# Gated linear attention by pairs of heads in one direction, with another order of the jobs

## The chip, the cores and the metric

One Trainium2 chip, one of its cores. The metric is the device time in microseconds from launch to end; it is given as the median of the runs shown, and a profile of one execution stands beside it.

## The reference

Two layers of one block, for 512 latent tokens (stream x) and 256 context tokens (stream c), width 1024. Each layer normalises and modulates the tokens, projects them with w_in, runs three mixers side by side, gates each of them, adds them and projects with w_out. The mixers are a convolution of width 31 (with a layer norm), a bidirectional gated linear attention, and grouped attention with 8 query heads. The change is in the linear attention: 4 heads with keys of 64 and values of 128, in chunks of 64 tokens, forwards and backwards:

```
cum = jnp.cumsum(log_a, axis=2)
last = cum[:, :, -1]
q_in = q * jnp.exp(cum)
k_in = k * jnp.exp(-cum)
att = jnp.where(mask, jnp.einsum('bnihd,bnjhd->bnhij', q_in, k_in), 0.0)
o_intra = jnp.einsum('bnhij,bnjhe->bnihe', att, v)
k_state = k * jnp.exp(last[:, :, None] - cum)
contrib = jnp.einsum('bnjhd,bnjhe->bnhde', k_state, v)
decay = jnp.exp(last)
# step over chunks: S <- decay * S + contrib
o_inter = jnp.einsum('bnihd,bnhde->bnihe', q_in, jnp.swapaxes(s_prev, 0, 1))
return (o_intra + o_inter).reshape(b_, t_, h_, dv), s_fin
```

The forward and the backward result are added, normalised, gated and projected with w_gla_out. Context tokens come first in both directions and pass their state on to the latent tokens. The second layer needs no output for the context.

## The kernel before, in words

The kernel is written as many small threads (Python generators) that a planner, the class Weaver (line 106), weaves into one order at build time. The planner keeps a clock for each engine from a price list (Engine.pe, line 251, and Engine.cost, line 273), takes the ready thread that can start first, and records its instructions; on the chip each engine then runs its list strictly in that order. All instructions pass through one helper, line 301, and DMAs through line 319, so that the profile names operations by tile and not by line.

The main thread runs a list of jobs, which the strings P["o0"] and P["o1"] write out by hand for the two layers (from line 78): q0 and q1 are the attention's projections, c0 to c7 the convolution's, v and k those of the linear attention (values; keys and queries), s0 to s11 the branch gates, m0 to m23 the merge gates, a and g (h in layer 1) the modulation of the next layer's input and of the outputs, and two digits a merge job (branch 0 convolution, 1 linear attention, 2 attention; then a block of columns). Projections split their fp32 operands into a high and a low part (hi and lo), in fp32r, and take three products. Loads of weights go ahead of the jobs as buffers become free: raw weights of projections (two buffers), and modulation weights in the general SBUF tiles r3 (29 of them, 128 x 768). Before any job, gates 8 and 9 (KOuter, line 595) run block by block as the first normalised inputs arrive.

PSUM has three pools of two buffers each: pg for projections and merges, pm for transposes, norms and readouts, p2 (double size) for attention and for the products of linear attention. The convolution is 31 multiply-adds over whole rows for each of 4 channel tiles, all on VectorE (tiles r, with the taps tp); it runs in a thread of low priority among everything else.

Linear attention starts when attention is over (gla_bias, line 1458): projections of values and of the low-rank gate, then log gates for all heads, one tile for each head with the 64 channels of the forward direction in partitions 0 to 63 and of the backward one in 64 to 127. The cumulative sum over time is two scans for each head, one of each half and one of them reversed (line 1526). Keys and queries (gla_qk_jobs, line 1533) leave PSUM four times for every projected tile of two heads and stream: each head's 64 rows are written to both halves of its own tile. Two lanes (gla_lane, line 1562) then take the four heads. For one head gla_head (line 1573) computes exponentials on ScalarE, the products with k and q on VectorE, transposes ks on TensorE, and then products (line 1654) issues the contributions of 14 chunks to the state (K=64 tokens, M=128, that is both directions in one product for chunks where both are wanted), and the masked attention blocks (K=64). VectorE updates the state chunk by chunk, 11 times for each direction on 64 partitions, forward and backward in turn (states, line 1629), and masks the blocks (intra, line 1640); GpSimd adds the two directions' blocks. The readout multiplies blocks by values, and queries of both directions at once (K=128) by the states, M=64 tokens at a time. gla_out (line 1700) normalises, transposes and stores to DRAM (ogd), from where the branch threads load it (tiles r from ogd; oad is the attention's).

Of the kernel before, what the change touches and what calls it, by code (L numbers as in the profile page):

```python
# [21 lines left out]
T = NC + NX  # L22
# [21 lines left out]
def _consts():  # L44
# [4 lines left out]
    for v in range(2):  # L49
        for g in range(4):  # L50
# [25 lines left out]
P = dict(vb=4, pko=12, res=2, resg=0, lead=6, pbr=2, tlead=3, nf=2, nbk=3, pconv=8, mlead=3, pmain=4, lcap=7,  # L76
         lcg=26, lat=6, vm=100, am=100, gm=104)
P["o0"] = (
    "c4 g0 m15 m1 q0 q1 m0 s3 s0 m16 m3 c2 m8 m10 m12 c0 k0 m14 c1 c3 m6 c5 k1 v0 m20 g1 s1 v1 c7 m4 k3 c6 "
    "m11 s2 m13 m19 m21 k2 m17 a3 s7 s6 m9 s10 s11 m22 m7 m23 m18 s5 a2 20 22 s4 a1 21 23 m5 m2 10 11 13 12 "  # L80
    "01 00 03 a0 02")
P["o1"] = (
    "q1 q0 c2 c5 c3 c6 m15 s1 s8 m14 s2 m22 m0 c1 c0 k1 m2 s0 s6 m5 m12 m20 s11 c4 c7 v1 s4 v0 s10 m9 s3 m6 "
    "h0 m4 m8 h1 k0 k2 m18 s9 m10 m7 s7 s5 k3 m23 m21 m17 m16 m1 22 23 m3 m13 20 m19 21 02 00 m11 03 10 11 12 "
    "01 13")
# [157 lines left out]
class Engine:  # L243
# [7 lines left out]
    def pe(self, name, a, k):  # L251
# [5 lines left out]
        else:  # L257
# [48 lines left out]
def hybrid_kernel(ctx: ExitStack, tc: tile.TileContext, x, c, ctx_in, c_ctx, norm_g, w_mod, b_mod,  # L306
# [452 lines left out]
    class Layer:  # L759
# [24 lines left out]
        def vec_loads(S):  # L784
# [9 lines left out]
            for d in range(2):  # L794
                o.append((vr[61:65, 64 * d:64 * d + 64], gla_b_gate[l, d].rearrange("(h d) -> h d", d=64)))
# [468 lines left out]
        def attn_pv(S, s, qp, h):  # L1264
# [18 lines left out]
            if S.cnt["attn"] == S.nunits:  # L1283
                W.res, W.lowcap = P["resg"], P["lcg"]
                W.low -= 2 * sum(d.get(2 * t) is not None for d in (S.kk, S.qq) for t in range(2))
# [172 lines left out]
        def gla_bias(S):  # L1458
# [63 lines left out]
            for h in range(GH):  # L1522
# [10 lines left out]
        def gla_qk_jobs(S):  # L1533
            S.kk, S.qq = {}, {}

            def dup(dst, t, col, key):
                def ev(s, cols, ps, fr):
                    if 2 * t not in dst:
                        dst[2 * t] = None
                        yield from (need(("r3", 2)) if "low" in dst else W.need_low(2))  # L1540
                        dst[2 * t], dst[2 * t + 1] = r3([T]), r3([T])
# [517 lines left out]
```

## Time and profile before

| | us |
|---|---|
| median of 3 runs (lowest, highest) | 1473.6 (1471.5, 1474.01) |
| the profiled execution's own time | 1471.48 |
| its span, first to last instruction | 1469.3 |
| TensorE busy, weight loads busy | 1401.7, 1196.5 |
| VectorE busy | 1118.8 |
| ScalarE busy | 597.3 |
| GpSimd busy | 237.8 |
| granted TensorE clock, mean share | 0.995 |

Shares of busy time are averages over a program that has two like halves, one for each layer. In the trace, layer 0's attention runs until about 357 us, its linear attention's heads from 541 to 664, its merges from 666 to 805; in layer 1 attention ends at 1131 us, the heads run from 1251 to 1347, the merges from 1317 to 1417. The page's PE row counts a matmul from its start to a modelled end; matmuls overlap in the array, so that a busy PE is not a PE at its peak. "Idle before" in a row is the time in which an engine stood still just before such instructions, and the name after the arrow is what ended it.

### The profile page before, as it was taken

The page shows a single profiled execution, that of the slowest core. Times are in us where ns is not written, and L with a number is a line of the kernel's source. Part 1 is how long each engine was busy: PE and PEld are TensorE (multiplying, and loading weights), DVE is VectorE, ACT ScalarE, POOL GpSimd, SP SyncE. Part 2 cuts the span into 40 slices and gives each one's busy share as a digit, 9 for nine tenths or more (in the row PEclk, how much of TensorE's full clock was granted, in tenths as well). Part 3 has the DMA queues.
Part 4 walks back from the last instruction along what each step waited for, and adds up shares of the span by engine and source line. Part 5 has one row for each costly group of instructions (what it writes and reads, how often), then busy time and mean ns, then how long its engine had stood idle before and what let it go on. Part 6 is the DMA issues. An engine that isn't in the chain of part 4 may idle for free.

```text
span 1469.3 us, 23375 instructions
## 1 busy us (share of the span) xinstructions
PE 1401.7 (95%) x8788; PEld 1196.5 (81%) x8788; DVE 1118.8 (76%) x1976; ACT 597.3 (41%) x1146; POOL 237.8 (16%) x333
## 2 busy tenths in 40 slices
PE   3999999999999999899999999999999999999998
PEld 2798888888998887787888777888888978778786
DVE  4434976778986999885858476886999999888664
ACT  4422465554225342333523164355554267432220
POOL 1001412221000003232050011412331000021200
PEclk9999999999999999999999999999999999999999
DMA  9732322112422622556556353242233173354752
GB/s 269 210 115 72 95 74 68 39 47 74 128 78 58 180 83 65 191 165 180 194 199 214 120 190 119 72 122 67 56 95 101 51 242 111 111 192 144 253 189 73
DMA packets 219365, 187.46 MB, mean 128 GB/s; under 512 B 15681, under 2 KB 182131, under 8 KB 219253
## 3 DMA queue, kind: packets, MB, share of 16 engines
q1 hardware_dynamic: 218948, 185.87, 41.1%
q8 instruction: 69, 1.13, 0.3%
q14 instruction: 44, 0.35, 0.1%
q10 hardware_dynamic: 304, 0.11, 0.0%
HBM read 151.86 MB, written 34.08 MB: 127 GB/s over the span
## 4 chain that ended last, share of the span: by engine, by line
PE 56%; DVE 10%; POOL 3%; ACT 2%; issue 2%; DMA 2%; SPq 1%; DVEq 0%; POOLq 0%; ACTq 0%
PE pg L301 43%; PE p L301 8%; DVE r L301 6%; PE pm L301 5%; POOL sm L301 2%; DVE wlo L301 2%; ACT r L301 1%; DMA r<-oad 1%; DVE sm L301 1%; SPq L319 1%; DVE tg L301 1%; DMA r<-thd 0%; ACT whi L301 0%; ACT tg L301 0%; DMA r<-in_w_mod 0%
## 5 line engine op out<-in xcount | busy, mean ns | idle before, releaser
L301 PE MATMUL pg<-hx,whi 128*128 128x512 f32 x1504 | 382.1, 397 | 1.6 <-DVE r L301 1.0
L301 PEld LDWEIGHTS pg<-hx,whi 128*128 128x128 f32 x1504 | 275.1, 189 | 57.2 <-issue 1.5
L301 DVE SCALAR_TENSOR_TENSOR r<-r,tp,r 128x768 f32<-128x768 f32 (+29 forms) x240 | 204.3, 902 | 0.2
L301 PE MATMUL pg<-hx,wlo 128*128 128x512 f32 x752 | 195.2, 393 | 0.0
L301 ACT CAST whi<-raw 128x512 fp32r<-128x512 f32 (+1 forms) x194 | 114.5, 620 | 187.7 <-PE pg L301 102.0
L301 DVE TENSOR_TENSOR wlo<-raw,whi 128x1024 fp32r<-128x1024 f32 (+1 forms) x140 | 173.0, 1236 | 17.2 <-ACT whi L301 14.4
L301 PEld LDWEIGHTS pg<-hx,wlo 128*128 128x128 f32 x752 | 138.6, 188 | 28.4 <-issue 0.8
L301 ACT ACTIVATE tg<-pg,hv 128x256 f32<-128x256 f32 (+1 forms) x116 | 71.7, 618 | 188.2 <-PE pg L301 163.4
L301 DVE TENSOR_TENSOR r<-r,r 128x512 f32<-128x512 f32 (+7 forms) x208 | 119.4, 600 | 19.0 <-DMA r<-ogd 8.0
L301 PE MATMUL pg<-r,whi 128*128 128x512 f32 (+1 forms) x576 | 125.7, 359 | 1.5 <-DVE r L301 1.4
L301 POOL TENSOR_SCALAR r<-r,sm 128x768 f32<-128x768 f32 (+1 forms) x80 | 81.4, 1019 | 278.1 <-DVE sm L301 207.9
L301 PEld LDWEIGHTS pg<-r,whi 128*128 128x128 f32 x576 | 95.9, 188 | 19.9 <-DVE r L301 2.6
L301 PE MATMUL pg<-hc,whi 128*128 128x256 f32 x768 | 107.2, 288 | 0.0
L301 PEld LDWEIGHTS pg<-hc,whi 128*128 128x128 f32 x768 | 99.4, 192 | 4.0 <-issue 0.7
L301 PE MATMUL p<-r,r 64*128 64x128 f32 (+2 forms) x672 | 90.5, 309 | 8.3 <-DVE r L301 6.0
L301 DVE TENSOR_TENSOR r<-p,r 128x384 fp32r<-128x384 f32 (+2 forms) x152 | 77.4, 543 | 27.1 <-ACT r L301 22.1
L301 ACT ACTIVATE r<-p,sm 128x768 f32<-128x768 f32 (+1 forms) x80 | 65.4, 818 | 70.5 <-DVE sm L301 65.5
L301 PEld LDWEIGHTS p<-r,r 64*128 64x128 f32 (+1 forms) x672 | 68.6, 189 | 22.5 <-issue 11.9
L301 PE MATMUL pm<-r,r 128*128 128x256 f32 (+4 forms) x672 | 83.3, 283 | 0.4 <-DVE r L301 0.4
L301 DVE CAST whi<-raw 128x512 fp32r<-128x512 f32 (+1 forms) x86 | 36.8, 429 | 60.3 <-PE pg L301 29.7
L301 PE MATMUL pg<-whi,hx 128*128 128x272 f32 (+2 forms) x480 | 82.2, 309 | 0.0
L301 POOL TENSOR_TENSOR r<-r,r 128x512 f32<-128x512 f32 (+1 forms) x33 | 45.2, 1375 | 220.4 <-DVE r L301 123.6
(166 smaller groups left out, 2180.7 us busy)
## 6 DMA issues: line engine op xcount, KB each, us to landing
raw<-in_w_in SPq DMA_DIRECT2D x116, 512.0 KB
r<-in_w_mod SPq DMA_DIRECT2D x64, 192.0 KB
thd<-tg SPq DMA_DIRECT2D x48, 256.0 KB
raw<-in_w_out SPq DMA_DIRECT2D x24, 512.0 KB
r<-thd SPq DMA_DIRECT2D x24, 384.0 KB
r<-in_w_mod SPq DMA_DIRECT2D x16, 384.0 KB
sgd<-tg SPq DMA_DIRECT2D x24, 256.0 KB
r<-thd SPq DMA_DIRECT2D x24, 256.0 KB
```

Source lines behind the costliest of these rows:

```text
L301: return real(*a, **k)
L319: (nc.scalar if q else nc.sync).dma_start(dst, src)
```

## The change

A tile now holds two heads of one direction. The log gates of heads 0 and 1 forwards are one tile, and so on: four tiles as before, with one scan for each over all 128 partitions. Keys and queries of a projected tile, which are two heads anyway, leave PSUM once for each stream, into one tile. gla_pair takes the place of gla_head: a pair of heads works on the two directions as two sets of tiles. The contributions have K=64 tokens and M=64 channels, one product for each head, 22 for each head and layer (8 forward, 8 backward, 6 of both in turn); the state updates run over 128 partitions, 22 for each pair, 8 of one direction in a row, 8 of the other, and 6 in turn. The readout has K=64 and M=64, separately for each direction. The second pair waits until the first one has issued its products (event pair0), and a readout takes both pm buffers at once. The planner's price list has a price for 64x64 products, its parameters P differ, and both job orders are new, of which the diff shows none but the parameters. What is quoted is the core; lines of it that go on alike are left out.

```diff
-P = dict(vb=4, pko=12, res=2, resg=0, lead=6, pbr=2, tlead=3, nf=2, nbk=3, pconv=8, mlead=3, pmain=4, lcap=7,
-         lcg=26, lat=6, vm=100, am=100, gm=104)
+P = dict(vb=4, pko=5, res=0, resg=1, lead=5, pbr=6, tlead=3, nf=3, nbk=4, pconv=13, mlead=3, pmain=4, lcap=11,
+         lcg=15, lat=6, vm=103, am=103, gm=121)
...
             elif rows <= 64:
-                c = 0.106 * n / 128
+                mode = (64, 64 if cols <= 64 else 128)
+                c = (0.06 if cols <= 64 else 0.106) * n / 128
             elif cols <= 64:
...
-                dma(w2r[16 * d:16 * d + 16, :, 64 * d:64 * d + 64],
-                    gla_w_gate[l, d].rearrange("r (h e) -> r h e", e=64))
+                dma(w2r[16 * d:16 * d + 16, 2 * d:2 * d + 2],
+                    gla_w_gate[l, d].rearrange("r (p c) -> r p c", c=128))
...
-            for h in range(GH):
+            for h in (0, 2, 1, 3):
                 yield "V"
                 V.tensor_sub(zn[h], cum[h], zn[h])
                 yield "V"
-                V.tensor_tensor_scan(cum[h][0:64], smask[0:64], zn[h][0:64], 0.0, op0=ALU.mult, op1=ALU.add)
-                V.tensor_tensor_scan(cum[h][64:128, ::-1], smask[64:128], zn[h][64:128, ::-1], 0.0,
-                                     op0=ALU.mult, op1=ALU.add)
+                if h < 2:
+                    V.tensor_tensor_scan(cum[h], smask, zn[h], 0.0, op0=ALU.mult, op1=ALU.add)
+                else:
+                    V.tensor_tensor_scan(cum[h][:, ::-1], smask, zn[h][:, ::-1], 0.0, op0=ALU.mult, op1=ALU.add)
...
-                            cp(dst[2 * t + e][64 * o:64 * o + 64, cols], ps[r], None, S.vv[r, col + t:col + t + 1])
+                    if t not in dst:
...
+                    cp(dst[t][:, cols], ps, None, S.vv[:, col + t:col + t + 1])
...
-                h = S.gq.pop(0)
-                yield from wait(S.E(("cum", h)), S.E(("kk", h)), S.E(("qq", h)))
-                yield from S.gla_head(h)
+                p = S.gq.pop(0)
+                if p:
+                    yield from wait(S.E("pair0"))
+                yield from wait(S.E(("cum", p)), S.E(("cum", 2 + p)), S.E(("kk", p)), S.E(("qq", p)))
+                yield from S.gla_pair(p)
...
+            yield from need(("r3", 6))
+            st = [[r3([6, 128]) for _ in range(2)] for _ in range(2)]
+            at = [r3([6, 128]) for _ in range(2)]
...
+            parts = ([(0, i) for i in range(8)], [(1, i) for i in range(8)], [(d, i) for i in range(8, 11) for d in range(2)])
+            chain = [_Event() for _ in parts]
...
+            def states(b, con):
+                if b == 2:
+                    yield from wait(chain[0], chain[1])
+                for n, (d, i) in enumerate(parts[b]):
+                    o = seq[d]
+                    yield "V" if n == 0 else "+V"
+                    V.scalar_tensor_tensor(ST(d, o[i + 1]), ST(d, o[i]), dec[d][:, o[i]:o[i] + 1], con[d, i],
+                                           op0=ALU.mult, op1=ALU.add)
                 free("p2")
...
             def products():
-                for b in range(max(len(groups), 2)):
-                    yield from need(("p2", (b < 2) + (b < len(groups))))
+                for b in range(3):
+                    yield from need(("p2", 1))
                     yield "P" if b == 0 else "+P"
...
+                    pcn = p2([2, 4, 128])
+                    cnt, con = [0, 0], {}
+                    for d, i in parts[b]:
+                        cix = seq[d][i]
+                        e = cix % 2
+                        con[d, i] = pcn[:, e, cnt[e]]
+                        cnt[e] += 1
+                        for a in range(2):
+                            PE.matmul(con[d, i][half[a]], lhsT=kt[d][half[e], cix // 2, half[a]],
+                                      rhs=gv[a][half[e], cix // 2], start=True, stop=True)
+                    spawn(states(b, con), 3)
                     if b < len(groups):
                         tts = groups[b]
-                        pa = p2([2, 4, 128])[:, :, 0:len(tts)]
+                        yield from need(("p2", 1))
+                        yield "+P"
+                        pa = p2([2, 4, 128])
                         for i, tt in enumerate(tts):
                             tk = slice(tt * 128, tt * 128 + 128)
...
+                            for d in range(2):
+                                for a in range(2):
+                                    PE.matmul(pa[:, a, 2 * d + i], lhsT=ki[d][half[a], tk], rhs=em[d][half[a], tk],
+                                              start=True, stop=True)
...
+                free("r3", 4)
+                fire(S.E(f"pair{p}"))
...
-                yield from need(("pm", 1))
+                yield from need(("pm", 2))
...
-                po = pm([nt, 128])
+                po = [pm([nt, 128]) for _ in range(2)]
...
-                    PE.matmul(po[:, i], lhsT=at[:, tt], rhs=gv[h][:, tt], start=(i == 0), stop=False)
-                for i, tt in enumerate(tts):
-                    for e in range(2):
-                        cix = 2 * tt + e
-                        PE.matmul(po[64 * e:64 * e + 64, i], lhsT=qq[h][:, cix * 64:cix * 64 + 64],
-                                  rhs=ST(cix, slice(0, 128)), start=False, stop=(i == nt - 1))
+                    for d in range(2):
+                        for a in range(2):
+                            for e in range(2):
+                                cix = 2 * tt + e
+                                PE.matmul(po[a][64 * e:64 * e + 64, i], lhsT=em[d][half[a], cix * 64:cix * 64 + 64],
+                                          rhs=ST(d, cix)[half[a]], start=False, stop=(i == nt - 1 and d == 1))
                 yield "+P"
-                spawn(S.gla_out(h, s, po, nt), 2)
+                for a in range(2):
+                    spawn(S.gla_out(2 * p + a, s, po[a], nt), 2)
```

Where the instructions stand, first on TensorE, in layer 0, at the products of the first head before (p_902 holds contributions, p_903 attention blocks, pg_ are projections; an x is a count of equal instructions):

```order
L301 MATMUL pg_5762<-hx_330,whi_5512 128x512
L301 MATMUL pg_5762<-hx_329,whi_5512 128x512
L301 MATMUL p_902_5778<-r_693_3978,r_873_5619 128x128 x8
L301 MATMUL p_903_5787<-r_858_5468,r_875_5621 128x128 x4
L301 MATMUL pg_5762<-hx_330,whi_5512 128x512
L301 MATMUL pg_5762<-hx_329,whi_5512 128x512
```

and at those of the first pair now, behind the 16 contributions of the forward chunks (p_881) and the first four of eight attention blocks (p_882); p_883 holds the backward chunks' contributions:

```order
L302 MATMUL p_882_5507<-r_835_5184,r_837_5186 128x128 x2
L302 MATMUL p_882_5507<-r_836_5185,r_838_5187 128x128 x2
L302 MATMUL pg_5470<-hx_331,whi_5271 128x512
L302 MATMUL pg_5470<-hx_330,whi_5271 128x512
L302 MATMUL pg_5470<-hx_331,whi_5271 128x512
L302 MATMUL pg_5470<-hx_330,whi_5271 128x512
L302 MATMUL pg_5470<-hx_331,whi_5271 128x512
L302 MATMUL pg_5470<-hx_330,whi_5271 128x512
L302 MATMUL pg_5470<-hx_331,whi_5271 128x512
L302 MATMUL pg_5470<-hx_330,whi_5271 128x512
L302 MATMUL pg_5470<-hx_331,whi_5271 128x512
L302 MATMUL p_883_5534<-r_714_4115,r_834_5183 64x128
```

Eight contributions of 128 rows became 16 of 64 rows, the blocks of two heads stand together, and nine matmuls of a projection stand between them and the next contributions, which come back to a p2 buffer that p_881 or p_882 must have left.

The state updates on VectorE at the same places, before (r_896 and r_897 are the states, mask the first blocks):

```order
L301 SCALAR_TENSOR_TENSOR r_896_5763<-r_896_5763,sm_5623,p_902_5778 64x128 x7
L301 SCALAR_TENSOR_TENSOR r_897_5764<-r_896_5763,sm_5623,p_902_5778 64x128
L301 SCALAR_TENSOR_TENSOR r_896_5763<-r_896_5763,sm_5623,p_902_5778 64x128
L301 SCALAR_TENSOR_TENSOR r_897_5764<-r_897_5764,sm_5623,p_902_5778 64x128
L301 SCALAR_TENSOR_TENSOR r_897_5764<-r_896_5763,sm_5623,p_902_5778 64x128
L301 SCALAR_TENSOR_TENSOR r_897_5764<-r_897_5764,sm_5623,p_902_5778 64x128
L301 COPY_PREDICATED zt_213<-mask,p_903_5787 128x512
```

and now:

```order
L302 SCALAR_TENSOR_TENSOR r_830_5151<-r_822_5081,tp_233,r_830_5151 128x773
L302 SCALAR_TENSOR_TENSOR r_873_5472<-r_873_5472,sm_5190,p_881_5488 128x128 x5
L302 SCALAR_TENSOR_TENSOR r_874_5473<-r_873_5472,sm_5190,p_881_5488 128x128
L302 SCALAR_TENSOR_TENSOR r_874_5473<-r_874_5473,sm_5190,p_881_5488 128x128 x2
L302 COPY_PREDICATED zt_213<-mask,p_882_5507 128x512
L302 COPY_PREDICATED zt_215<-mask,p_882_5507 128x512
L302 SCALAR_TENSOR_TENSOR r_820_5055<-r_406_2369,tp_233,r_820_5055 128x774
L302 SCALAR_TENSOR_TENSOR r_875_5474<-r_875_5474,sm_5191,p_883_5534 128x128 x3
```

Twelve updates of one head, forward and backward in turn, became eight of two heads in one direction; conv taps (tp) stand between the chains.

The loads on SyncE's queue at the start, before (w_mod 128x3x128 x2 is a modulation load of layer inputs, 128x3x256 one of an output gate; each of the two forms stands six and three times for a job):

```order
L319 DMA r_112_596<-in_w_mod 128x3x128 x2
L319 DMA r_113_599<-in_w_mod 128x2x128 x2
L319 DMA r_114_605<-in_w_mod 128x3x256
L319 DMA r_115_607<-in_w_mod 128x3x256
L319 DMA r_116_609<-in_w_mod 128x2x256
L319 DMA r_127_704<-in_w_mod 128x3x256
L319 DMA r_128_706<-in_w_mod 128x3x256
L319 DMA r_129_708<-in_w_mod 128x2x256
L319 DMA cst<-in_k_const 128x512
```

and now:

```order
L320 DMA r_113_599<-in_w_mod 128x2x128 x2
L320 DMA r_114_605<-in_w_mod 128x3x128 x2
L320 DMA r_115_608<-in_w_mod 128x3x128 x2
L320 DMA r_116_611<-in_w_mod 128x2x128 x2
L320 DMA r_128_705<-in_w_mod 128x3x128 x2
L320 DMA r_129_708<-in_w_mod 128x3x128 x2
L320 DMA r_130_711<-in_w_mod 128x2x128 x2
L320 DMA r_131_718<-in_w_mod 128x3x256
L320 DMA r_132_720<-in_w_mod 128x3x256
L320 DMA r_133_722<-in_w_mod 128x2x256
L320 DMA r_145_820<-in_w_mod 128x3x256
L320 DMA r_146_822<-in_w_mod 128x3x256
```

Six loads of job a2 moved ahead of those of the output gate (g0 before, g1 now) and of the constants.

## Rows read from the trace of the kernel before

**Rows 1.** The page: busy us, share and count, and busy tenths in 40 slices.
```profile
PE 1401.7 (95%) x8788; PEld 1196.5 (81%) x8788; DVE 1118.8 (76%) x1976; ACT 597.3 (41%) x1146; POOL 237.8 (16%) x333
...
PE   3999999999999999899999999999999999999998
...
DVE  4434976778986999885858476886999999888664
```

**Rows 2.** Windows: busy us (count) of each engine, granted clock, DMA share, GB/s.
```profile
450.00:540.00 90.00, 89.00 (x562) 78.10 (x561) 80.74 (x92) 39.47 (x65) 0.40 (x2) 1.00 0.39 113
540.00:620.00 80.00, 71.42 (x513) 61.04 (x512) 73.19 (x126) 26.83 (x48) 20.96 (x35) 0.96 0.36 116
620.00:700.00 80.00, 75.14 (x607) 63.14 (x606) 58.23 (x122) 29.55 (x53) 21.61 (x37) 1.00 0.56 173
...
1240.00:1320.00 80.00, 76.12 (x460) 61.81 (x459) 67.84 (x128) 37.88 (x65) 10.10 (x21) 0.98 0.50 153
```

**Rows 3.** Waits of 540:700 and 1240:1320 (us, times, longest), and the timeline's PE.
```profile
PE p L301 <- DVE r L301: 7.1, 4, 3.6
...
PE pm L301 <- DVE t L301: 4.2, 4, 2.0
...
PE p L301 <- DVE r L301: 2.5, 2, 1.9
...
617.49 1.51 PE L301 MATMUL p<-cst,r 128*128 128x128 f32 x6 [3.63 <-DVE r L301]
...
669.78 0.63 PE L301 MATMUL pm<-cst,tg 128*128 128x128 f32 x4 [2.00 <-DVE t L301]
```

**Rows 4.** PE groups by form: count, busy us, mean ns, idle before; last, the chain.
```profile
L301 PE MATMUL pg<-hx,whi 128*128 128x512 f32 x1504 | 382.1, 397 | 1.6 <-DVE r L301 1.0 <-ACT tg L301 0.6
...
L301 PE MATMUL p<-r,r 64*128 64x128 f32 x384 | 27.7, 286 | 5.5 <-DVE r L301 4.9 <-DVE zt L301 0.5
...
L301 PE MATMUL pg<-r,cstat 128*32 128x128 f32 x768 | 26.2, 286 | 5.0 <-DMA r<-in_w_mod 5.0
...
L301 PE MATMUL pm<-r,r 128*128 128x128 f32 x80 | 11.6, 284 | 0.0
L301 PE MATMUL pm<-r,r 128*64 128x128 f32 x160 | 11.4, 280 | 0.0
...
1442.12 2.75 PE pg L301 x12
```

**Rows 5.** Groups by form on VectorE and ScalarE.
```profile
L301 DVE SCALAR_TENSOR_TENSOR r<-r,sm,p 64x128 f32<-64x128 f32 x176 | 60.8, 346 | 5.7 <-PE p L301 0.6
...
L301 DVE TENSOR_TENSOR_SCAN r<-r,r 64x768 f32<-64x768 f32 x16 | 28.0, 1749 | 0.2
...
L301 DVE TENSOR_TENSOR r<-pg,r 128x128 f32<-128x128 f32 x48 | 11.7, 289 | 0.8 <-PE pg L301 0.6
...
L301 DVE TENSOR_SCALAR r<-pg,vv 64x512 f32<-64x512 f32 x9 | 6.7, 749 | 8.3 <-ACT r L301 8.3
...
L301 DVE TENSOR_SCALAR r<-pg,vv 64x256 f32<-64x256 f32 x7 | 3.4, 484 | 1.7 <-ACT r L301 1.2 <-PE pg L301 0.4
...
L301 DVE COPY sm<-r 64x12 f32<-64x12 f32 x16 | 2.6, 165 | 0.1
...
L301 ACT ACTIVATE r<-pg,vv 64x512 f32<-64x512 f32 x23 | 15.7, 683 | 19.8 <-PE pg L301 12.8 <-DVE r L301 6.8
...
L301 ACT ACTIVATE r<-pg,vv 64x256 f32<-64x256 f32 x17 | 8.0, 470 | 5.2 <-PE pg L301 4.0 <-DVE r L301 1.1
```

**Rows 6.** The first 80 us: GB/s in 40 slices of 2 us; the timeline's PE from 62 us.
```profile
GB/s 8 181 284 227 239 251 283 319 343 298 302 285 291 284 304 312 312 312 294 285 301 281 284 302 290 295 293 340 313 379 271 21 0 0 0 8 44 218 0 66
...
62.40 2.16 PE L301 MATMUL pg<-hc,whi 128*128 128x256 f32 x16
...
69.02 1.98 PE L301 MATMUL pg<-hx,wlo 128*128 128x512 f32 x8
70.92 1.30 PE L301 MATMUL pg<-r,cstat 128*32 128x128 f32 x40
```

More of the change, by code (lines that the diff above doesn't have):

```diff
@@ L1284, in attn_pv @@
                 W.res, W.lowcap = P["resg"], P["lcg"]
-                W.low -= 2 * sum(d.get(2 * t) is not None for d in (S.kk, S.qq) for t in range(2))
+                W.low -= sum(d.get(t) is not None for d in (S.kk, S.qq) for t in range(2))
                 S.kk["low"] = S.qq["low"] = True
@@ new lines, in gla_pair @@
+            q0, qs, kk, qq = S.q0, S.qs, S.kk[p], S.qq[p]
+            gv = S.gv[2 * p:2 * p + 2]
+            half = (slice(0, 64), slice(64, 128))
+            yield from need(("r3", 6))
+            ks, em, ki = ([r3([T]) for _ in range(2)] for _ in range(3))
+            lc, dec = [sm() for _ in range(2)], [sm() for _ in range(2)]
+            for d in range(2):
+                cu = S.cum[2 * d + p]
+                c3 = cu.rearrange("p (n c) -> p n c", c=CH)
+                yield "V"
+                V.tensor_copy(lc[d][:, :NCH], c3[:, :, 0 if d else CH - 1])
+                yield "V"
+                V.tensor_sub(ks[d].rearrange("p (n c) -> p n c", c=CH), c3,
+                             lc[d][:, :NCH].rearrange("p (n o) -> p n o", o=1).to_broadcast([128, NCH, CH]))
@@ new lines, in gla_pair @@
+            yield "S"
+            free("r3", 4)
+            kt = [k.rearrange("p (t d) -> p t d", d=128) for k in ks]
+            for d in range(2):
+                yield from need(("p2", 1))
+                yield "P" if d == 0 else "+P"
+                pk = p2([8, 128])
+                for tt in range(6):
+                    PE.transpose(pk[:, tt], ks[d][:, tt * 128:(tt + 1) * 128], K["ident"])
+                yield "E"
+                cp(kt[d], pk[:, 0:6])
+                free("p2")
@@ L1623, in gla_head, with ST @@
+            yield "S"
+            yield from need(("r3", 6))
+            st = [[r3([6, 128]) for _ in range(2)] for _ in range(2)]
+            at = [r3([6, 128]) for _ in range(2)]
+            def ST(d, cix):
+                return st[d][cix // 6][:, cix % 6]
+            G.memset(ST(0, 0), 0.0)
+            G.memset(ST(1, NCC - 1), 0.0)
+            seq = (list(range(NCH)), list(range(NCC - 1, -1, -1)) + list(range(NCH - 1, NCC - 1, -1)))
             done_a = _Event()
-            blks = ([0, 1, 2, 3, 11, 10, 4, 5], [9, 8, 7, 6, 5, 10])
@@ L1626, in gla_head @@
             groups = [S.qtt[g:g + 2] for g in range(0, len(S.qtt), 2)]
-            chain = [_Event(), _Event()]
-            def states(b, pcn, con, i0, i1):
-                if b:
-                    yield from wait(chain[0])
-                for i in range(i0, i1):
-                    for o, r in ((fo, F_), (bo, B_)):
-                        yield "V" if (i == i0 and r == F_) else "+V"
-                        V.scalar_tensor_tensor(ST(o[i + 1], r), ST(o[i], r), dec[r, o[i]:o[i] + 1], con[o[i]][r],
-                                               op0=ALU.mult, op1=ALU.add)
+            parts = ([(0, i) for i in range(8)], [(1, i) for i in range(8)], [(d, i) for i in range(8, 11) for d in range(2)])
@@ L1667, in products @@
                     if b < len(groups):
                         tts = groups[b]
-                        pa = p2([2, 4, 128])[:, :, 0:len(tts)]
+                        yield from need(("p2", 1))
+                        yield "+P"
+                        pa = p2([2, 4, 128])
                         for i, tt in enumerate(tts):
                             tk = slice(tt * 128, tt * 128 + 128)
-                            for d, r in enumerate((F_, B_)):
-                                PE.matmul(pa[:, d, i], lhsT=ki[r, tk], rhs=qq[h][r, tk], start=True, stop=True)
```

151 lines of the change are left out of this document (57 added, 94 removed).

## The prediction

> **What bounds the kernel now.** I read the page's busy times first. TensorE (PE) is busy 95% of the span, VectorE (DVE) 76%, ScalarE (ACT) 41% [rows 1]. That looks like a TensorE-bound kernel in which no other engine matters, but two views correct it. In the slices, PE is at 8 or 9 tenths everywhere after the first one, and DVE is at 9 only in some slices [rows 1]. The windows put those beside the stages: in 540 to 620 us, where layer 0's linear attention runs, PE is busy 71.42 of 80 us while DVE is busy 73.19; in 620 to 700 us PE has 75.14 of 80; in layer 1's linear attention, 1240 to 1320 us, PE has 76.12 of 80 and DVE 67.84 [rows 2]. So PE idles 8.6 + 4.9 + 3.9 us there. The waits name the cause: in 540 to 700 us PE waits 7.1 us for DVE on tiles r and 4.2 us on tiles t, in 1240 to 1320 us 2.5 us on r [rows 3]; the longest, 3.63 us at 617.49, is the transposes of a head waiting for the product of ks and k on DVE [rows 3].
>
> The second correction is that busy is not full pace. The commonest matmul (128x512, 1504 records) takes 382.1 / 1504 = 254 ns of busy time each, but where the chain of waits runs undisturbed 12 of that size take 2.75 us, 229 ns each [rows 4]. About a tenth of PE's busy time is thus slack that the busy share does not show.
>
> **The array's work.** Each fp32 matmul leaves two records. Before, a head and layer has 14 contributions with K=64, M=128 (8 + 6), two attention blocks per token tile with K=64, M=128, and two readouts of the state per token tile with K=128, M=64. Over 4 heads and 2 layers (6 token tiles in layer 0, 4 in layer 1) that is 112, 80 and 80 matmuls, as the counts x384 (112 + 80, doubled) and x160 say [rows 4]. After, a pair has 22 contributions for each of its two heads with K=64, M=64: 176; the readouts have K=64, M=64 and are split by direction: 160; the attention blocks stay at 80. So 224 + 160 records become 352 + 320 = 672. The old ones cost 27.7 / 384 = 72 ns and 11.4 / 160 = 71 ns of busy time per record, 16.2 + 11.4 = 27.6 us together. The trace has no 64x64 product. The two bounds: 72 ns, as for a half-sized product now, gives 672 x 72 = 48.4, +20.8 us; the modulation products, which stand four beside each other in quarters of the columns (128x32), cost 26.2 / 768 = 34 ns per record [rows 4], and give 22.8, -4.8 us. I take -5, since the trace goes by the share of the array: the full-sized fp32 products take 11.6 / 80 = 145 ns per record, the half-sized 72 and the quarters 34 [rows 4]. A 64x64 product is a quarter, and the loops alternate the two heads (two column halves or two row halves) as the modulation alternates its quarters.
>
> The Trainium skill ("TensorE: Matmul & The Clock Gate", section "Wait — 56ns, not 53.3ns?") has a rule against this: with hardware decode off the sequencer spends about 62 ns per matmul, and that becomes the bound once the array's work is shorter. By it 672 records would cost 41.7 us, +14 instead of -5. The modulation row, 34 ns per record over 768 records, disagrees with it for this kernel.
>
> **VectorE and ScalarE.** States: 176 updates of 64 partitions at 346 ns (60.9 us) become 88 of 128 partitions with the same 128 elements per partition. Duration goes by elements per partition: a 128x128 addition from PSUM takes 289 [rows 5]. Bounds 289 and 346 ns; I take 346: 30.4 us saved (35.5 at the other end). Scans: 16 of 64x768 at 1749 ns become 8 of 128x768: 14.0 us. Copies of the last column: 16 become 8 at 165 ns: 1.3 us. The evacuation of k and q: 56 instructions on half the partitions (DVE 6.7 + 3.4 us, ACT 15.7 + 8.0 us [rows 5]) become 14 on all: a quarter of 33.8 us, 25.3 us saved, 7.6 on DVE and 17.7 on ACT at the old split. DVE is relieved of 53 us in all, about half in each layer; products with the gates, masks, transposes and norms keep their number.
>
> What of it lies on the path? Only where PE waits for DVE. All but the states and some of the scans of layer 0 stand before 540 us, where DVE is busy 80.74 of 90 and PE waits 1 us [rows 2]; a faster DVE shifts its later work forward there, conv taps above all, which run among the heads. With some 26 us less in front of it per layer, DVE reaches the heads' products earlier than PE by more than the waits named, so I let them go: 7.1 + 4.2 - 2.0 = 9.3 us in layer 0 (2.0 us is counted below) and 2.5 in layer 1. The array's granted clock was 0.96 of 2.4 GHz in 540 to 620 us and 0.98 in 1240 to 1320 [rows 2], after these idle stretches; at its other level, 1.2 GHz, that is 3.2 + 1.6 = 4.8 us of lost pulses, which I count as won back. Together -17 us, ends 0 and -22 (all 17.4 us of idle time in the three stretches and the clock). What is late next is the loads: branch products on DVE wait for oad and ogd, and POOL's chain of small operations behind each head's norm is unchanged.
>
> **Waits that the pairs add.** The second pair waits for the first one's products, and each chain of 8 updates now runs in one direction, each update reading what the last one wrote. Queued behind on PE are the next contributions, which need the PSUM buffer of the chain before last. The order puts 8 attention blocks and 9 matmuls of 229 ns between: about 3.2 us, against 8 x 346 = 2.8 us of updates. I cost this at nothing; without that cover (a DVE that is busy with conv taps when the products land) it is up to 2.8 us at each of 8 chains, 22 us. SBUF buffers: a pair asks for 6 + 6 where two heads asked for 3 + 3 each, and k and q hold 4 instead of 8; no cost.
>
> **The order of jobs.** At the start two jobs of modulation now stand before the first projection, a2 and g1, where c4 and then g0 stood. SP sends a2's 2 x 2 x 8 x 128 x 128 x 4 bytes, 2.1 MB, more before the constants. The loads ran at some 290 GB/s until 62 us [rows 6], so g1 arrives 7 us later, at about 69. Before, c4 ran from 62.40 to 71.0 us and g0's products began at 70.92 [rows 6]. Now PE must hold m21 until g1 is through, at 71, and has only a2's 64 records (1.95 us) and the rest of gates 8 and 9 to fill the 8.6 us that c4 filled: +5 us, between 0 (if the loads land sooner) and +8. At the end of layer 0, a0 stood among the last merges, and its transposes waited 2.00 us for a linear-attention output to leave its bank [rows 3]; now a0 runs in the middle of the layer: -2. All other moves I cost at nothing, with +-8, since PE has projections left to run beside the heads in both orders.
>
> **Sum:** -5 -17 +5 -2 = -19 us on the profiled execution's 1471.5 us (span 1469.3, 2.2 around it): 1452.5. The median of the runs shown stands 2.1 above that execution: 1454.6, so I say 1455.
>
> **Rivals.** (a) More is won. If PE's pace improves too in the stages where DVE fell behind, a further 15 to 20 us can go: the commonest form alone holds 1504 x 25 ns = 38 us. For it: DVE is near 90% over long stretches; against: half of that slack lies in stages that the change leaves alone. 1455 - 18 = 1437. (b) No change: what PE waited for at the heads is POOL's norm chain and the loads, which come as late as before, and the start takes 5 us: 1455 + 17 = 1472. For it: both stand behind the heads in the trace; against: the waits name DVE. (c) Slower: the 64x64 products cost as much each as the half-sized ones now, because four do not run beside each other. Place: contributions and readouts; price 72 instead of 34 ns per record: 1455 + 26 = 1481. It decides from 34 + 19 / 0.672 = 62 ns on, where the gain is gone. For it: the trace has no product that splits rows and columns at once; against: the rows of 145, 72 and 34 ns. By the skill's 62 ns the time would be 1455 + 19 = 1474, no change; the row of 34 ns speaks against it. (d) Slower by order: the chains of 8 are not covered (22 us) and start and boundaries lose as much as the heads win: 1455 + 24 = 1479.
>
> **How the numbers follow.** My forecast (1445 to 1466) has 0.50, (a) 0.23, (b) 0.09 with the skill's rule 0.02 of it, (c) 0.08, (d) 0.10. No change means within 0.2%, 3 us, about what a measurement of this kernel can tell. Faster: 0.50 + 0.23 = 0.73; same 0.09; slower 0.18. The likeliest case's time is 1455. The range takes in (a) down to 1430 and (d) up to its 1479; (c) and the far edges, under 0.2, stay out.
>
> **What would show it.** In the changed profile: 672 records of M=64 with 23 us of busy time, and not 48; 88 state updates of about 346 ns and 8 scans of 1.75 us; DVE busy about 1065 us; PE idle in the two linear-attention stages down from 17 us to about 5 with a clock of 0.99 or more; first projection at about 71 us. I am wrong if PE still waits for DVE by 10 us there, if DVE's relief is there but PE's idle time has moved to another stage, or if the records of M=64 cost over 60 ns.

## The result and the profile after

The changed kernel takes 1438.7 us (median of 4 runs, 1437.5 to 1439.5) against 1472.6 us (4 runs, 1471.1 to 1474.0) before, beside it on the same chip: a ratio of 0.9765, 95% interval 0.9753 to 0.9778. It is 34 us faster; the forecast was 18.6 us under the 1473.6 shown, 1455, with 1430 to 1479 as its range. The sign and the range held, and the size is that of rival (a).

The profiled execution has a span of 1435.7 us where before it was 1469.3. The page of the changed kernel, busy times and slices of PE, DVE and the granted clock:

```profile
PE 1384.6 (96%) x9076; PEld 1187.9 (83%) x9076; DVE 1059.7 (74%) x1863; ACT 574.3 (40%) x1113; POOL 233.8 (16%) x325
...
PE   3999999999999999999999999999999999999998
...
DVE  4437966689946999963676485877679999997664
...
PEclk9999999999999999999999999999999999999999
```

Against [rows 1], VectorE has 59.1 us less to do and ScalarE 23.0. TensorE's busy time fell by 17.1 us and its idle time (span less busy) from 67.6 to 51.1, by 16.5: together the 33.6 us of span. The mean granted clock rose from 0.995 to 1.000.

The groups by form that answer to [rows 4] and [rows 5]; the last line is the modulation, which the price of a quarter of the array was taken from:

```profile
L302 PE MATMUL p<-r,r 64*64 64x128 f32 x352 | 12.4, 275 | 2.9 <-DVE r L302 2.9
...
L302 PE MATMUL pm<-r,r 64*64 64x128 f32 x320 | 10.1, 273 | 0.0
...
L302 DVE SCALAR_TENSOR_TENSOR r<-r,sm,p 128x128 f32<-128x128 f32 x88 | 28.8, 343 | 2.7 <-PE p L302 0.9
...
L302 DVE TENSOR_TENSOR_SCAN r<-r,r 128x768 f32<-128x768 f32 x8 | 14.0, 1750 | 0.0
...
L302 PE MATMUL pg<-r,cstat 128*32 128x128 f32 x768 | 26.4, 286 | 4.8 <-DVE t L302 4.2 <-DMA r<-in_w_mod 0.6
```

The 672 records of 64x64 products cost 12.4 + 10.1 = 22.5 us, 33.5 ns each. Their mean length in the row, 275 ns, is the time that one is under way and not its cost, since several are under way at once: the busy time over the count is what is to be read.

Windows of the changed kernel. The heads of layer 0 now run from 495 to 613 us, those of layer 1 from 1231 to 1294, so the stretches that answer to [rows 2] lie earlier; the columns are the same:

```profile
405.00:495.00 90.00, 90.00 (x617) 81.20 (x615) 57.99 (x87) 38.05 (x62) 0.35 (x2) 1.00 0.38 113
495.00:575.00 80.00, 76.10 (x677) 65.60 (x676) 76.63 (x107) 23.94 (x45) 22.34 (x33) 1.00 0.48 134
575.00:655.00 80.00, 77.98 (x677) 66.07 (x676) 62.19 (x134) 40.61 (x65) 19.19 (x35) 1.00 0.49 154
1220.00:1300.00 80.00, 75.05 (x665) 60.49 (x664) 73.16 (x132) 32.27 (x53) 20.89 (x33) 1.00 0.41 130
```

PE idles 3.9 + 2.0 + 5.0 = 10.9 us in the three stretches of the heads, where it was 17.3; the clock is 1.00 in all. PE's waits there, first of 495 to 655, then of 1220 to 1300 us (us in total, times, longest):

```profile
PE pm L302 <- DVE t L302: 3.2, 6, 0.9
PE p L302 <- DVE r L302: 1.4, 3, 0.7
...
PE pm L302 <- DVE t L302: 1.5, 2, 1.3
PE p L302 <- DVE r L302: 1.5, 3, 1.0
PE pm L302 <- POOL r L302: 1.0, 1, 1.0
```

In layer 0 the waits for r went from 7.1 to 1.4 us and the longest from 3.6 to 0.7, against [rows 3]. What is left is many short waits.

### The profile page after: what moved, and what is told of

It is laid out like the page before. It is cut to its first block, busy times and chain, and to the rows that moved or that the text cites. A ratio compares the mean times of both kernels' runs of the same rounds, so it can differ in the third digit from the quotient of the medians.

```text
span 1435.7 us, 23778 instructions
## 1 busy us (share of the span) xinstructions
PE 1384.6 (96%) x9076; PEld 1187.9 (83%) x9076; DVE 1059.7 (74%) x1863; ACT 574.3 (40%) x1113; POOL 233.8 (16%) x325
## 4 chain that ended last, share of the span: by engine, by line
PE 50%; DVE 5%; POOL 1%; issue 1%; ACT 1%; DMA 0%; SPq 0%; DVEq 0%; POOLq 0%
PE pg L302 36%; PE p L302 9%; PE pm L302 4%; DVE r L302 3%; POOL sm L302 1%; DVE tg L302 1%; DVE wlo L302 1%; DVE t L302 0%; DMA r<-oad 0%; DVE zt L302 0%; POOL r L302 0%; ACT r L302 0%; ACT tg L302 0%; DVE sm L302 0%; ACT whi L302 0%
## 5 line engine op out<-in xcount | busy, mean ns | idle before, releaser
L302 PE MATMUL pg<-hx,whi 128*128 128x512 f32 x1504 | 385.8, 397 | 0.3 <-DVE r L302 0.3
L302 DVE SCALAR_TENSOR_TENSOR r<-r,tp,r 128x768 f32<-128x768 f32 (+29 forms) x240 | 201.2, 883 | 0.2
L302 DVE TENSOR_TENSOR wlo<-raw,whi 128x1024 fp32r<-128x1024 f32 (+1 forms) x140 | 173.7, 1241 | 17.1 <-ACT whi L302 16.2
L302 DVE TENSOR_TENSOR r<-r,r 128x512 f32<-128x512 f32 (+8 forms) x208 | 119.1, 599 | 24.7 <-DMA r<-ogd 9.0
L302 DVE TENSOR_TENSOR r<-p,r 128x384 fp32r<-128x384 f32 (+2 forms) x152 | 77.8, 544 | 33.8 <-ACT r L302 27.6
L302 PE MATMUL p<-r,r 64*64 64x128 f32 (+3 forms) x800 | 84.8, 299 | 4.1 <-DVE r L302 2.9
L302 POOL TENSOR_TENSOR r<-r,r 128x512 f32<-128x512 f32 (+1 forms) x33 | 48.3, 1469 | 224.3 <-DVE r L302 219.4
L302 PE MATMUL pm<-r,r 128*128 128x256 f32 (+3 forms) x832 | 81.4, 279 | 0.2
L302 PEld LDWEIGHTS p<-r,r 64*64 64x64 f32 (+2 forms) x800 | 65.7, 163 | 17.5 <-issue 7.4
```

The lines of the kernel that those rows point to most:

```text
L302: return real(*a, **k)
```

## Experiments: the layout or the order

One theory says that the pairs win the time by themselves, because VectorE is relieved and the array's products get cheaper; the other, that the new order of jobs does.

**The pairs with the old orders.** In the changed kernel the planner's numbers and the two orders are those of before, except lcg:

```
 P = dict(vb=4, pko=12, res=2, resg=0, lead=6, pbr=2, ...
-         lcg=26, ...
+         lcg=15, ...
```

> The pairs with the job orders and the planner's numbers of before, but for one: the tiles that projections may reserve beside linear attention are cut from 26 to 15, since a pair asks for six at once and the old number leaves it none. Theory 1, the layout brings the gain (53 us less on VectorE, which TensorE waited for): at least half of the 34 us, 1440 to 1456 us. Theory 2, the new order brings it: 1465 to 1480 us.

Measured: 1454.8 us (1453.9 to 1457.2), 0.9868 of before [0.9852, 0.9884]; before stood at 1474.8 beside it. So the pairs alone bring 20 us. Its span is 1452.1 us with PE busy 1392.0: 17.2 us less span than before, 7.5 of it idle and 9.7 busy time. The granted clock is 0.999 over the span. Its page:

```profile
PE 1392.0 (96%) x9076; PEld 1188.9 (82%) x9076; DVE 1063.8 (73%) x1879; ACT 567.9 (39%) x1097; POOL 233.6 (16%) x325
```

**The old heads with the new orders and numbers.** The kernel before, with all of P, o0 and o1 of the change.

> The heads of before with all numbers and both job orders of the changed kernel. Theory 1 (layout): 1462 us or more, since VectorE keeps its 1119 us of work. Theory 2 (order): 1438 to 1452 us.

Measured: 1515.7 us (1515.2 to 1518.3), 1.0284 [1.0265, 1.0303]. PE waits for DVE's t 22.1 us and for r 17.8. The new orders are worth nothing without the pairs.

**Orders and numbers apart.** Three kernels with the pairs: the old orders with the new numbers; the new orders with the old numbers (lcg 15); the new numbers and layer 0's new order with layer 1's old one.

> The changed kernel with the two job orders of before and the planner's numbers of the change. With the numbers of before as well (but for lcg, 15 as in the change) the pairs alone took 1454.8 us, 0.987 of before; the whole change took 0.9765. Some 15 us are therefore left for orders and numbers together. If the orders win them, this run stays at 1450 to 1457; if the numbers do (the priority pko of the gate products, the queue depths nf, nbk, pbr, pconv and the planner's scale of each engine's durations), it comes out at 1437 to 1443.

> The changed kernel with its own two job orders and the planner's numbers of before (but for lcg, 15 as in the change). If the orders win the 15 us that the pairs alone leave open, 1437 to 1443; if the numbers do, 1450 to 1457; if an order is only good with the numbers that it was made for, worse than the pairs with old orders and old numbers, over 1458.

> The changed kernel with layer 1's order of before; layer 0's order and the numbers are the change's. In the two traces the stretch from the end of layer 1's attention to the end of the program is 338 us in both, and layer 0's linear attention ends 51 us earlier after the change. If layer 1's order has no part in the gain, 1436 to 1442. If it wins half of what orders and numbers win together, about 1446. If the two orders are matched to each other (jobs of layer 1 fill PE while layer 0's heads run), 1450 or more.

Measured, before at 1474.0: 1462.4 us (0.9919 [0.9902, 0.9936]), 1560.8 us (1.0599 [1.0570, 1.0629]) and 1443.9 us (0.9795 [0.9780, 0.9809]). The new numbers alone lose 8 us against the pairs with everything old, the new orders alone lose 106, and both together win 16. The first theory's ranges held in both of the first runs, but by themselves the pairs bring only some 20 of the 34 us. The rest comes neither from the new orders nor from the new numbers alone, but only from both together, as one plan made for the pairs. In the run with 1560.8 (the profiled execution took 1568.8), PE waits 44.9 us for ScalarE's r, 23.4 of it between 1000 and 1100 us, where layer 1's attention runs and PE is busy only 69.8 of 100 us. Layer 1's order is worth 5 us of the 16.

Where the plan's 16 us lie shows in windows of 100 us. First the pairs with the old orders, then the change:

```profile
0.00:100.00 100.00, 73.59 (x669) 60.80 (x670) 40.82 (x125) 41.33 (x80) 3.89 (x13) 1.00 0.75 214
100.00:200.00 100.00, 96.81 (x564) 84.39 (x564) 65.28 (x136) 34.43 (x81) 25.19 (x42) 1.00 0.28 77
...
1300.00:1400.00 100.00, 95.68 (x477) 77.23 (x476) 59.12 (x78) 28.98 (x50) 18.78 (x20) 1.00 0.60 197
```

```profile
0.00:100.00 100.00, 75.23 (x696) 60.92 (x697) 40.16 (x126) 39.87 (x77) 3.77 (x12) 1.00 0.81 235
100.00:200.00 100.00, 99.12 (x634) 88.76 (x633) 78.84 (x175) 43.95 (x111) 29.29 (x51) 1.00 0.25 70
...
1300.00:1400.00 100.00, 99.86 (x438) 81.27 (x437) 65.69 (x89) 33.37 (x57) 16.41 (x13) 1.00 0.64 216
```

PE's busy time is 4.0 us more in the first 200 us and 4.2 more from 1300 to 1400, in layer 1's merges, where the pairs with the old orders wait for DVE's branch products. Their timeline of PE there:

```profile
1317.15 2.12 PE L302 MATMUL pg<-r,whi 128*128 128x512 f32 x8 [2.70 <-DVE r L302]
...
1352.20 2.14 PE L302 MATMUL pg<-r,whi 128*128 128x512 f32 x8 [1.62 <-DVE r L302]
```

Neither place is the heads. With the old orders the windows of the heads are these:

```profile
540.00:620.00 80.00, 76.84 (x709) 63.96 (x708) 70.09 (x130) 40.39 (x69) 23.87 (x41) 1.00 0.39 120
620.00:700.00 80.00, 76.93 (x638) 65.71 (x637) 45.42 (x95) 24.40 (x42) 13.39 (x28) 1.00 0.68 213
...
1230.00:1310.00 80.00, 77.37 (x671) 62.69 (x671) 58.28 (x108) 26.07 (x45) 16.88 (x34) 1.00 0.48 145
```

PE idles 3.2 + 3.1 + 2.6 = 8.9 us in them, less than the change's 10.9. Of the 16.4 us between the spans of the two profiles, 9.0 are idle time of PE and 7.4 busy time. The rest of the idle time is spread over the span, and no single wait carries it; beyond some 1.5 us of clock (0.999 against 1.000) no row says where the busy time went.

## Experiments: what is on the path

These kernels are the change with every instruction in its place (the planner reckons with the change's own durations, so that the order stays), and one thing issued more often or left out. The edits are quoted in short form; alt hands the planner the change's own instruction and issues the listed ones in its place. The runs are set against the change's 1438.7; the kernel before stood 1 to 2 us higher beside them than beside the change, so that a difference of 2 us means nothing here.

**The array.** Each contribution product is issued twice, 352 records more.

```
-  PE.matmul(con[d, i][half[a]], lhsT=kt..., rhs=gv..., start=True, stop=True)
+  one = (...the same operands...)
+  PE.alt("matmul", [one, one], ...)
```

> The changed kernel in its own order, with every contribution product issued twice in a row: 352 more records of M=64, K=64 at 35 ns, 12.4 us of TensorE. If TensorE's list is now what sets the end, the time goes up by 9 to 13 us, to 1448 to 1452 us; if TensorE still waits at the heads, the added products fall into the waits and it goes up by 0 to 5 us.

Measured: 1446.4 us, 0.9806 [0.9789, 0.9822], +7.7 us. PE's busy time is 1396.9, 12.3 more: the products cost what they cost once (35 ns a record), and two thirds of it reach the end.

**VectorE's updates and scans in halves.** Every state update and scan of 128 partitions becomes two of 64, as many as before the change:

```
-  V.scalar_tensor_tensor(ST(d, o[i + 1]), ST(d, o[i]), dec..., con[d, i], ...)
+  for r in half:
+      V.scalar_tensor_tensor(ST(d, o[i + 1])[r], ST(d, o[i])[r], dec...[r], con[d, i][r], ...)
-  V.tensor_tensor_scan(cum[h], smask, zn[h], ...)
+  for r in half:
+      V.tensor_tensor_scan(cum[h][r], smask[r], zn[h][r], ...)
```

> The changed kernel in its own order, instruction for instruction, but each state update and each scan is issued as two halves of 64 partitions, as before the change. VectorE has 88 more updates of 346 ns and 8 more scans of 1.75 us, 44 us in all; nothing else differs. Theory 1 (TensorE's gain is VectorE's relief): 15 to 35 us more, 1454 to 1474 us. Theory 2 (the order hides the heads wherever VectorE stands): under 8 us more.

Measured: 1488.8 us, 1.0097 [1.0082, 1.0112], +50 us, more than either theory expected, with VectorE at 1109.1 (+49.4). Then the same with the planner told of it:

> The state updates and scans are again issued as two instructions of 64 partitions each, as in the run with the order held fixed (+50 us against the change for +49 us of VectorE work), but now the planner is told of them and sets every instruction's place anew. If the VectorE work itself is what binds in the linear-attention stages, no order hides it: 1470 to 1490, with VectorE at about 1109 us and PE waiting for r and t as in the run before the replanning. If most of the loss came from an order that counted on shorter updates, the planner wins it back: 1445 to 1460.

Measured: 1489.3 us, 1.0104 [1.0089, 1.0119]. Replanning with the same orders and numbers wins nothing back. Next, which of the two kinds it is: the updates alone in halves, and, for load outside the chains, each scan four times.

```
-  V.tensor_tensor_scan(cum[h], smask, zn[h], ...)
+  V.alt("tensor_tensor_scan", 4 * [...the same...], ...)
```

> The changed kernel, every instruction in its place, but the 88 state updates issued as two halves of 64 partitions (176 instructions as before the change, about +30 us of VectorE work, all of it inside the chains of 8 updates). With updates and scans in halves the loss was 50 us. If VectorE's load as such binds, the loss here is that load, about 30 us (1468), and the scans bear the other 20. If it is the chains, whose 8 steps then outlast the matmuls that cover them and stop PE eight times, nearly all of the 50 us are here: 1480 or more. If both together were needed, under 1455.

> The changed kernel, every instruction in its place, but each of the 8 scans issued four times in a row (+24 x 1.75 = 42 us of VectorE work, 21 in each layer, ahead of the chains and outside them). If VectorE's load as such binds up to the linear attention, +35 to +42 us (1473 to 1481). If only what stands in the chains counts, and work ahead of them is taken up by VectorE's idle time (it is busy 74% of the span), +0 to +12 us (1438 to 1451).

Measured, before at 1474.7: 1479.3 us (1.0033 [1.0022, 1.0043]), +40.5, and 1478.4 us (1.0028 [1.0017, 1.0039]), +39.6. In the run with the updates in halves, the waits of PE of 480 to 700 us, and then two lines of DVE's timeline with the line of PE's that follows the second:

```profile
PE p L309 <- DVE r L301: 9.5, 4, 3.6
PE pm L309 <- DVE t L309: 4.2, 2, 4.0
PE pm L309 <- DVE r L309: 3.2, 1, 3.2
...
513.59 4.50 DVE L301 SCALAR_TENSOR_TENSOR r<-r,sm,p 64x128 f32<-64x128 f32 x12
...
589.93 6.03 DVE L301 SCALAR_TENSOR_TENSOR r<-r,sm,p 64x128 f32<-64x128 f32 x16 [0.29 <-PE p L309]
...
596.02 1.10 PE L309 MATMUL p<-r,r 64*64 64x128 f32 x32 [3.11 <-DVE r L301]
```

A chain of 16 halves takes 6.03 us, and the contributions behind it wait 3.11 us, until it is done. This is rival (d)'s mechanism; in the change itself it costs 2.9 us in all, the idle time before its 352 contribution records. The same place in the changed kernel, DVE and then PE:

```profile
579.83 3.03 DVE L302 SCALAR_TENSOR_TENSOR r<-r,sm,p 128x128 f32<-128x128 f32 x8 [0.30 <-PE p L302]
...
583.01 1.10 PE L302 MATMUL p<-r,r 64*64 64x128 f32 x32 [0.20 <-DVE r L302]
```

There the 8 updates take 3.03 us and PE waits 0.20. With the updates in halves four such waits stand in each layer, 9.5 and 10.1 us: half of the 40.5; beside them stand waits for t and other tiles r, and a granted clock that fell to 0.91 in 495 to 575 us. That run alone does not part load from chains. The run with the scans does, since its chains are untouched. Its windows, and its waits of PE of 400 to 500 and of 1180 to 1340 us:

```profile
405.00:495.00 90.00, 81.93 (x554) 73.96 (x552) 60.49 (x79) 30.97 (x51) 0.35 (x2) 0.96 0.32 93
...
1220.00:1300.00 80.00, 62.06 (x427) 49.64 (x426) 76.75 (x106) 25.44 (x46) 9.94 (x18) 0.89 0.32 91
```

```profile
PE pg L309 <- ACT tg L309: 11.4, 2, 6.1
...
PE pg L309 <- DVE wlo L309: 10.3, 1, 10.3
PE p L309 <- DVE r L309: 6.6, 4, 4.2
```

42 us of VectorE work ahead of the chains came back as 39.6 us. PE stands for 11.4 us before the heads, where the change has no idle time at all, and 10.3 us for wlo, a weight's low half that VectorE makes: a projection, and no part of linear attention. VectorE and ScalarE run their lists in order (the timelines of this run show the change's sequence), so that a late scan makes everything behind it late. The 11.4 us are put down to ScalarE's tg, but ScalarE itself had stood 10.80 us for a tile that VectorE made behind its third scan. The line of ScalarE's timeline, then the run's page:

```profile
485.58 0.84 ACT L309 ACTIVATE r<-r 128x768 f32<-128x768 f32 x1 [10.80 <-DVE r L309]
...
PE 1397.7 (95%) x9076; PEld 1196.7 (81%) x9076; DVE 1099.9 (75%) x1887; ACT 575.0 (39%) x1113; POOL 233.0 (16%) x325
```

That an us costs about an us is not waiting alone. Of the 40.1 us that the span is longer, 27.0 are idle time of PE and 13.1 busy time, at a granted clock of 0.987 where the change has 1.000; with the updates in halves it is 27.3 and 14.7, also at 0.987. And the scans stand where VectorE has hardly a gap, whatever its mean share of 74%. The changed kernel, around its scans:

```profile
455.00:495.00 40.00, 40.00 (x240) 35.47 (x238) 37.01 (x43) 18.98 (x32) 0.00 (x0) 1.00 0.31 93
1193.00:1250.00 57.00, 55.57 (x420) 46.31 (x419) 55.05 (x87) 20.73 (x38) 3.95 (x5) 1.00 0.38 108
```

VectorE is free for 3.0 of 40 and 2.0 of 57 us there. What an us of its work costs in other stretches was not tried.

**Less load.** The scans are left out, so that the running sums, and all that follows from them, are not computed.

> The changed kernel, every instruction in its place, with the 8 scans of the log-decays left out (the running sums along time are not computed, so the decays and all that follows from them differ), 14.0 us of VectorE work less. It tells what more relief of VectorE would bring now. If its load still sets the pace of the linear-attention stages, another 10 to 14 us: 1425 to 1429. If PE is now fed in time and the rest is the loads, the start and the planner's order: 1434 to 1439.

Measured: 1440.9 us, 0.9772 [0.9751, 0.9794]: nothing won (+2). So under this order, at and just ahead of the heads, 35 to 49 us more of VectorE's busy time cost 40 to 50 us, and 12.5 us less of it gave nothing. Between the change's own load and those 35 us more there is a knee; where, smaller additions would have shown.

**The evacuation.** Each evacuation of k and q is issued as four instructions of 64 partitions.

```
-  cp(dst[t][:, cols], ps, None, S.vv[:, col + t:col + t + 1])
+  for r in 2 * [slice(0, 64), slice(64, 128)]:
+      cp(dst[t][r, cols], ps[r], None, S.vv[r, col + t:col + t + 1])
```

> The changed kernel, every instruction in its place, but each evacuation of k and q issued as four instructions of 64 partitions (56 as before the change: two halves, twice) instead of one of 128 (14). It gives back some 25 us of work, two thirds on ScalarE and a third on VectorE. If that work was hidden, as ScalarE's 40% busy share suggests, within 5 us of the change's 1438.7. If the PSUM bank that each product holds until it is evacuated is what counts, or the 7 to 10 us on VectorE count as the states do, 1445 to 1460.

Measured: 1446.5 us, 0.9810 [0.9790, 0.9830], +7.8. The work went to ScalarE (598.7 us busy, +24.4) and hardly to VectorE (+1.4), so a third of ScalarE's part is on the path although that engine is 40% busy; PE idles 6.9 us more, in no single wait. Whether by the PSUM banks held longer or by other work of ScalarE that came later was not tried.

## Why the prediction was right in sign and short in size

**The array, -5: right.** 672 records at 33.5 ns cost 22.5 us against 22.8 reckoned, and 27.6 before: -5.1. Rival (c) needed 72 ns and is out. The Trainium skill ("TensorE: Matmul & The Clock Gate", section "Wait — 56ns, not 53.3ns?") states about 62 ns per matmul for the case that hardware decode is off; an estimate by it, record by record, is 41.7 us, and the row shows 22.5. The prediction put that rule aside by the modulation row, also counted by records; but a matmul of the program leaves two, and an estimate by the 336 matmuls is 20.8 us, which the row does not rule out. No run shows which count is the right one, or how the kernel's matmuls are decoded.

**VectorE's relief: the work right, a little more than said.** 88 updates at 343 ns, 8 scans at 1750 ns; VectorE's busy time fell by 59.1 us where 53 was reckoned. 1.8 of the 6 are the evacuation, of which VectorE now has one instruction of 14 (0.7 us, and not 2.5), and 1.6 the updates, which partly overlap now (28.8 us is less than 88 x 343 ns). The sum also took an update's duration for its cost: by the lines above 16 halves take 6.03 us, so that the 176 of before held VectorE for some 66 us and not for 61. ScalarE's relief, reckoned as 17.7 us (its busy time fell by 23.0), was not priced at all: the run with four instructions for each evacuation puts it at 7.8 us under the new plan.

**What of it lies on the path, -17: nearly right for the layout.** With the old orders the pairs gave -17.2 us of span: 5.1 the array; the clock, reckoned as 4.8 us and by its means worth (1 - 0.995) x 1469 = 7 us before and 1.5 with the pairs; and 7.5 us of idle time where 11.8 had been named. The step "I let them go" was too generous: the named waits shrank, but others took part of their place, and in the three stretches PE idles 8.9 us with the old orders and 10.9 in the change, and not 5. Layout terms of -5 - 17 = -22 stand against -20 measured by medians. How these 20 divide between VectorE, ScalarE and the array was reckoned and not measured under the old order. Of the 17.1 us by which PE's busy time fell in the whole change, 5.1 are the array and some 7 the clock; no row names the other 5.

**The order: this step failed.** The forecast took "+5" for the start, "-2" for a0 and "all other moves I cost at nothing". The runs put the new plan at -16 us for the pairs. The start shows one reason. The first projection did come late, at 69 us and not at 62, as reckoned; but PE had more to do meanwhile than "a2's 64 records and the rest of gates 8 and 9": the timeline of PE in the changed kernel runs through, with the gates' products (p) up to 67 us, and 75.23 us of work in the first 100 against 73.99 before.

```profile
60.74 1.95 PE L302 MATMUL pg<-r,cstat 128*32 128x128 f32 x64
62.62 0.51 PE L302 MATMUL p<-hc,whi 128*128 128x256 f32 x2
...
67.15 0.39 PE L302 MATMUL p<-hx,wlo 128*128 128x512 f32 x1
67.47 1.95 PE L302 MATMUL pg<-r,cstat 128*32 128x128 f32 x64
69.35 2.17 PE L302 MATMUL pg<-hc,whi 128*128 128x256 f32 x16
```

Before, part of these products ran after the first projection. A job that comes first only moves work, as long as PE has other work that is ready.

The deeper error was to hold the order for a list of moves that each have a price. What the runs show is a plan that fits the pairs, wins at the start and in layer 1's merges rather than at the heads, and is worth nothing without the pairs (1515.7) or without its own numbers (1560.8). Why this plan is better for the pairs than the old one, job by job, was not settled.

Rival (a) had the size by luck and not the reason. It took 254 against 229 ns for the commonest matmul as a slower pace that could be won back. But a form's busy time also counts the end of each group that already runs beside the next form. In the changed kernel's timeline 12 such matmuls are busy 2.91 us, 243 ns each, and the next form starts 2.75 us after they did, 229 ns each:

```profile
1077.60 2.91 PE L302 MATMUL pg<-hx,whi 128*128 128x512 f32 x12
1080.35 1.57 PE L302 MATMUL pm<-r,r 128*128 128x256 f32 x12
```

The shorter the groups, the more such ends there are: the forms of the kernel before add up to some 1650 us, where its page has PE busy for 1401.7. After the change that form shows 385.8 us for its 1504 records where it showed 382.1, 257 ns each: none of the 38 us was won.

**The added waits at nothing: nearly right.** PE waits 1.4 and 1.5 us for r in the two stages; the chain's cover of some 3.2 us all but holds against 3.03. There is nothing to spare: with twice the steps it fails eight times.

**Layer 1: less than said.** From the end of its attention (1131 us before, 1098 after) to the end of the program the span has 338 us in both traces, so that the layer's second half is no shorter. The clock in its heads did rise from 0.98 to 1.00, but of the 2.5 us of waits for r 1.5 are left and others came in: PE idles 5.0 of the 80 us there, where it was 3.9.

## What to carry to other kernels

Ask of a relieved engine where the knee is: here 55 us taken off a VectorE that was 76% busy, with 29 off ScalarE and 5 off the array, brought 17 to 20 under the old order; in the new order 35 to 49 us put back at the heads cost about one each and a further 14 taken off gave nothing. Mean shares and named waits had not shown that; the busy share of the stretch just ahead of the heads does. A layout's time is the time of layout and order together, so measure the new layout with the old order and the old layout with the new one before the gain is put down to either. An update or a scan on half the partitions costs as much as one on all of them (346 against 343 ns, 1749 against 1750), so cut tiles so that every lane has work.

## What was not expected of the hardware

Updates in halves of 64 partitions gain nothing from being independent of their neighbours. In the run with the updates in halves, neighbours work on different partitions, and 16 still take 6.03 us, 377 ns each. With 128 partitions, 8 that each read what the last one wrote take 3.03 us, 379 ns each; but where the two directions alternate, so that no update reads its neighbour's result, 6 take 1.62 us in all. The changed kernel's DVE timeline:

```profile
507.47 1.62 DVE L302 SCALAR_TENSOR_TENSOR r<-r,sm,p 128x128 f32<-128x128 f32 x6
```

With durations of 0.34 us, independent updates on all partitions thus overlap by some 0.09 us ((6 x 0.34 - 1.62) / 5), and those on halves did not. That both halves write one tile is not the reason: in the 12 halves at 513.59 us of that run the two directions, which have tiles of their own, take turns, so that 5 of the 11 neighbours write different tiles, and they still take 4.50 us, 375 ns each. Neighbouring halves always lie on different halves of the partitions; whether that change or the half itself keeps them apart was not tried.
